# Strassen's seven products in the feed-forward part of the last two token blocks of a decoder layer

## The chip, the core and the metric

The kernel runs on one core of a Trainium2 chip. Its time is device microseconds of one execution. TensorE (PE) multiplies, VectorE (DVE), ScalarE (ACT) and GpSimd (POOL) work element by element, and every transfer is issued by SyncE (SP), one instruction after the other. Each engine takes its instructions in the order in which the program has them.

## What is computed

One decoder layer on 2048 tokens of width 1024, in float32:

```python
h = rms_norm(x, pre_mix_norm)
q, k, v_a, u, v_s = split(h @ w_in)                  # 512 columns each
attn = dilated_mixture_attention(rotary(q), rotary(k), v_a)
sgu = spatial_gating(u, v_s, ...)
y = concatenate([rms_norm(attn), rms_norm(sgu)]) @ w_out
x = x + rms_norm(y, post_mix_norm)
h = rms_norm(x, pre_ffn_norm)
f = (silu(h @ w_gate) * (h @ w_up)) @ w_down         # 1024 -> 2816 -> 1024
x = x + rms_norm(f, post_ffn_norm)
```

## The kernel before

Tokens are worked on in four blocks of 512 (m = 0 to 3). Every matrix product is made three times over in a reduced float format, `F32R`: an operand is split into a high part (a copy that rounds, on ACT) and a low part (what is left, a subtraction on DVE), and high by high, high by low and low by high are added up in PSUM. So each step of 128 in the contraction costs three matmuls of 128x512 where one would do otherwise. `wtile` (L143) loads 256 KB of a weight and splits it: `w_raw` has 3 buffers, `w_hi` and `w_lo` have 4 (`W_SPL`). `group` (L180) multiplies into four PSUM banks: for each step of the contraction it loads and then multiplies for banks 0 to 3; the last `tail` steps are turned round, so that all of them are finished for bank 0, then for bank 1 and so on, and each bank is evacuated as soon as it is done.

The program has three stretches.

1. The input projections of all blocks, with the attention of blocks 0 and 1 (`heads(0)`) interleaved.
2. Output projection and feed-forward part of blocks 0 and 1, with the attention of blocks 2 and 3 (`heads(1)`) interleaved. `merge` takes steps from both generators in a fixed ratio, 318 of the one to 252 of the other. `ffn_up` (L967) writes its result to DRAM (`fD`), and `ffn_down` (L1014) reads it back and splits it (`fsplit`, L1007, two buffers) beside the weight.
3. `out_proj(2)`, `out_proj(3)`, `ffn_prep(2)`, then the feed-forward part of blocks 2 and 3 with nothing beside it but the preparation of block 3. Here the activations stay in SBUF in split form.

`out_rows` (L861) finishes a projection: each bank goes through ACT (sum of squares) and DVE (times the gain) into `y`, which has 2 buffers in all. After the second half, for each of eight tiles of 128x512 the residual `xr` is loaded, added by DVE and the row is written out. With one `xr` buffer (`XR = 1`) the next residual is asked for when the one before has been used. `out_proj(3)` uses the same `y`, `ah` and `al` buffers as `out_proj(2)`. For the last block (`late`) the residuals are loaded early and each bank's rows are finished as soon as the bank is; there `tail` is 4.

The order on each engine is made by a scheduler that follows the program and its priorities; it can move an instruction ahead of others where buffers and data allow.

Of the kernel before, what the change touches and what calls it, by code (L numbers as in the profile page):

```python
# [10 lines left out]
F32 = mybir.dt.float32  # L11
# [15 lines left out]
NFF = DFF // P  # L27
KT = DM // P
# [45 lines left out]
LATE_TAIL = 4  # L74
# [9 lines left out]
W_SPL = 4  # L84

# [8 lines left out]
class Body:  # L94
    def __init__(self, tc, ctx, t):
# [3 lines left out]
        self.psd = ctx.enter_context(tc.tile_pool(name="psd", bufs=4, space=PSUM))  # L99
        self.psq = ctx.enter_context(tc.tile_pool(name="psq", bufs=2, space=PSUM))  # L100
        self.psv = ctx.enter_context(tc.tile_pool(name="psv", bufs=2, space=PSUM))
        self.wp = ctx.enter_context(tc.tile_pool(name="wp", bufs=1))
        self.tiny = ctx.enter_context(tc.tile_pool(name="tiny", bufs=1))
# [10 lines left out]
        self.fD = [d.tile([NFF, P, TB], F32, name=f"fD{m}") for m in range(NM)]  # L114
# [14 lines left out]
    def rstd(self, ss, n, inv_n, eps, name, parts=P):  # L129
        v = self.nc.vector  # L130
        a = self.tiny.tile([parts, n], F32, name=name + "_a", tag="rs_a", bufs=2, padded_shape=[P, 32])
        y = self.tiny.tile([parts, n], F32, name=name + "_y", tag="rs_y", bufs=6, padded_shape=[P, 32])
# [10 lines left out]
    def wtile(self, src, perm=False, shape=None, save=None, pool=None, bufs=None):  # L143
# [3 lines left out]
        raw = self.wp.tile([P, 512], F32, name="w_raw", tag="w_raw", bufs=W_RAW)  # L147
# [17 lines left out]
    def wcached(self, src, saved, perm):  # L165

        raw = self.wp.tile([P, 512], F32, name="w_raw", tag="w_raw", bufs=W_RAW)
# [56 lines left out]
    def consts(self, pool):  # L224
        self.cst = self.const.tile([P, C_TRIL], F32, name="cst")
        self.cs0 = pool.tile([P, C_W - C_TRIL], F32, name="cs0")
        self.dma(self.cs0, self.t["consts"][:, C_TRIL:C_W])
# [139 lines left out]
    def ip_keep(self, m):  # L367

        for k in range(KT):
            for i in range(2):  # L370
                self.dma(self.hD[k, i], self.h[m][i][k])
                yield
        self.dma(self.cst, self.t["consts"][:, 0:C_TRIL])
# [166 lines left out]
    def attn_pools(self, pool):  # L540
        self.ap = pool

# [314 lines left out]
    def ff_pools(self, pool, fpool):  # L857
        self.fp = pool
        self.fpool = fpool

    def out_rows(self, m, n_k, load, ops, res, gain, dst, keep, late=False):  # L861

        nc, v, pool = self.nc, self.nc.vector, self.fp
        y = [pool.tile([P, 4, 512], F32, name="y", tag="y", bufs=2) for _ in range(2)]
# [9 lines left out]
        todo = [(n, j) for j in range(4) for n in range(2)] if late else [(n, j) for n in range(2) for j in range(4)]  # L874

        def fetch(i):
            if i < 8:
                n, j = todo[i]
                tag, bufs = ("ah", KT) if late else ("xr", XR)
                xs[i] = pool.tile([P, 512], F32, name="xr", tag=tag, bufs=bufs)  # L880
                self.dma(xs[i], res[j * P:(j + 1) * P, 512 * n:512 * n + 512])

        def row(i, r):
# [6 lines left out]
            if not late:  # L890
                fetch(i + XR)

        if late:
            for i in range(8):
                fetch(i)
        for n in range(2):
            def evac(b, ps, n=n):
                nc.scalar.activation(self.junk, ps, AF.Square, accum_out=ss[:, n, b:b + 1])
                v.tensor_tensor(y[n][:, b, :], ps, grow[n], ALU.mult)  # L899
                if late and n == 1:  # L900
                    v.tensor_tensor(ss[:, 0, b:b + 1], ss[:, 0, b:b + 1], ss[:, 1, b:b + 1], ALU.add)
                    r = self.rstd(ss[:, 0, b:b + 1], 1, 1.0 / DM, RMS_EPS, "po")
                    row(2 * b, r)
                    row(2 * b + 1, r)

            yield from self.group(n_k, lambda k, n=n: load(k, n), ops, evac, tail=LATE_TAIL if late and n == 1 else 2)
        if not late:
            for i in range(XR):
                fetch(i)
            v.tensor_tensor(ss[:, 0, :], ss[:, 0, :], ss[:, 1, :], ALU.add)  # L910
            r = self.rstd(ss[:, 0, :], 4, 1.0 / DM, RMS_EPS, "po")
            for i, (n, j) in enumerate(todo):
                row(i, r[:, j:j + 1])
        if keep:
            v.tensor_tensor(sk[:, 0, :], sk[:, 0, :], sk[:, 1, :], ALU.add)
            r1 = self.rstd(sk[:, 0, :], 4, 1.0 / DM, RMS_EPS, "pk")
            self.r1[m] = self.tiny.tile([P, 4], F32, name="r1", tag="r1", bufs=NM)
            v.tensor_copy(self.r1[m], r1)
        yield

    def ffn_mid(self, m, nxt):

        if nxt is None:
            yield from self.ffn_down(m)
        else:
# [240 lines left out]
```

## Time and profile before

| | |
|---|---|
| median of 3 runs | 2553.68 us (2550.77 to 2557.73) |
| profiled execution | 2557.3 us, span 2555.5 us |
| PE busy | 2384.9 us (93% of the span), 10817 matmuls |
| DVE busy | 1551.2 us (61%) |
| ACT busy | 1156.2 us (45%) |
| POOL busy | 52.2 us (2%) |
| DMA | 439.36 MB, mean 172 GB/s |
| mean granted clock of PE | 0.964 |

The span runs from the first to the last instruction of the profiled execution. The granted clock is the share of TensorE's 2.4 GHz that the throttle let through; 0.5 of it is the lower of its two levels, 1.2 GHz. Matmuls overlap, so the length of one in a row (0.39 us) is more than the distance from one start to the next.

### The profile page before, as it was taken

What the parts mean: (1) busy time and instruction counts of PE and PEld (TensorE: products, weight loads), DVE (VectorE), ACT (ScalarE), POOL (GpSimd) and SP (SyncE); (2) the same over time, 40 slices, a digit from 0 to 9 for tenths busy, and PEclk for the clock granted to TensorE, in tenths of its full rate; (3) what the DMA queues carried; (4) which work ended last, traced back from release to release, by engine and by line L of the source; (5) the groups of instructions that cost most, each with busy time, mean ns of one, the idle gap of its engine ahead of it and who ended that gap; (6) DMA issues with size and microseconds to landing.
All of it is one profiled execution on the core that took longest, in us unless ns stands there. A gap on an engine that the chain in (4) does not pass through costs nothing.

```text
span 2555.5 us, 32840 instructions
## 1 busy us (share of the span) xinstructions
PE 2384.9 (93%) x10817; PEld 1940.0 (76%) x10817; DVE 1551.2 (61%) x3249; ACT 1156.2 (45%) x2095; POOL 52.2 (2%) x174
## 2 busy tenths in 40 slices
PE   7998869889897999999999999986999999999998
PEld 6776758767675788887788888775788888888886
DVE  5427788885786995768888575664533323533323
ACT  6425755664544653445545354443533323333321
POOL 0000000000000000000000000000000000000000
PEclk9998979889998999999999999998999999999999
DMA  7877757777866654566665445665633323533432
GB/s 243 294 218 240 224 166 225 250 219 240 259 187 182 211 159 139 142 193 184 190 202 146 125 136 178 192 218 174 185 96 95 95 92 114 157 94 95 126 101 91
DMA packets 336251, 439.36 MB, mean 172 GB/s; under 512 B 29488, under 2 KB 187728, under 8 KB 335568
## 3 DMA queue, kind: packets, MB, share of 16 engines
q1 hardware_dynamic: 336080, 437.27, 55.9%
q8 instruction: 85, 1.39, 0.2%
q14 instruction: 86, 0.70, 0.1%
HBM read 359.35 MB, written 77.80 MB: 171 GB/s over the span
## 4 chain that ended last, share of the span: by engine, by line
PE 74%; DVE 9%; DMA 9%; ACT 4%; SPq 2%; issue 2%; DVEq 0%; ACTq 0%; POOL 0%
PE d L188 67%; SPq L127 2%; DMA xr<-in_x 2%; PE qk L704 2%; PE qk L705 1%; PE pv L787 1%; PE pv L785 1%; DMA w_raw<-in_w_in 1%; DVE w_lo L160 1%; DVE y L886 1%; DVE io L427 1%; DMA xs<-in_x 1%; DMA xr<-x 1%; PE qk L313 1%; DMA w_raw<-in_w_out 0%
## 5 line engine op out<-in xcount | busy, mean ns | idle before, releaser
L160 DVE TENSOR_TENSOR w_lo<-w_raw,w_hi 128x512 fp32r<-128x512 f32 x632 | 434.1, 688 | 579.9 <-ACT w_hi L159 577.7
L159 ACT CAST w_hi<-w_raw 128x512 fp32r<-128x512 f32 x632 | 390.5, 619 | 711.0 <-PE d L188 615.0
L188 PE MATMUL d<-ah,w_hi 128*128 128x512 f32 x1408 | 556.5, 396 | 2.1 <-ACT ah L315 2.1
L188 PE MATMUL d<-ah,w_lo 128*128 128x512 f32 x1408 | 556.8, 395 | 0.0
L188 PE MATMUL d<-al,w_hi 128*128 128x512 f32 x1408 | 556.6, 395 | 0.0
L188 PEld LDWEIGHTS d<-ah,w_hi 128*128 128x128 f32 x1408 | 264.2, 188 | 62.1 <-ACT ah L315 2.6
L188 PEld LDWEIGHTS d<-ah,w_lo 128*128 128x128 f32 x1408 | 264.3, 188 | 61.6
L188 PEld LDWEIGHTS d<-al,w_hi 128*128 128x128 f32 x1408 | 264.4, 188 | 60.7
L188 PE MATMUL d<-w_hi,fh 128*128 128x512 f32 x704 | 279.4, 397 | 1.8 <-ACT fh L1011 1.8
L188 PE MATMUL d<-w_hi,fl 128*128 128x512 f32 x704 | 275.7, 395 | 3.8 <-DVE fl L1012 3.8
L188 PE MATMUL d<-w_lo,fh 128*128 128x512 f32 x704 | 278.6, 396 | 0.0
L188 PE MATMUL d<-w_hi,hh 128*128 128x512 f32 x384 | 155.5, 411 | 7.2 <-DVE io L427 5.0
L188 PEld LDWEIGHTS d<-w_hi,fl 128*128 128x128 f32 x704 | 132.1, 189 | 35.0 <-DVE fl L1012 6.8
L188 PEld LDWEIGHTS d<-w_hi,fh 128*128 128x128 f32 x704 | 133.4, 189 | 31.6 <-ACT fh L1011 3.5
L188 PE MATMUL d<-w_lo,hh 128*128 128x512 f32 x384 | 156.2, 407 | 0.0
L188 PEld LDWEIGHTS d<-w_lo,fh 128*128 128x128 f32 x704 | 133.4, 190 | 28.2
L188 PE MATMUL d<-w_hi,hl 128*128 128x512 f32 x384 | 154.3, 404 | 0.0
L188 PE MATMUL d<-w_hi,ah 128*128 128x512 f32 x256 | 105.7, 414 | 35.9 <-DVE y L899 35.9
L810 DVE TENSOR_TENSOR pl<-S,ph 128x512 fp32r<-128x512 f32 (+1 forms) x160 | 99.2, 624 | 45.3 <-ACT ph L809 26.5
L785 PE MATMUL pv<-ph,v 128*128 128x256 f32 (+1 forms) x344 | 95.4, 293 | 30.5 <-ACT ph L809 22.7
L808 ACT ACTIVATE S<-S 128x512 f32<-128x512 f32 (+1 forms) x160 | 89.5, 579 | 50.6 <-DVE S L800 43.4
L188 PE MATMUL d<-hh,w_hi 128*128 128x512 f32 x256 | 103.0, 407 | 9.6 <-DVE io L427 7.8
(206 smaller groups left out, 3623.4 us busy)
## 6 DMA issues: line engine op xcount, KB each, us to landing
w_raw<-in_w_gate SPq DMA_DIRECT2D x176, 256.0 KB
w_raw<-in_w_up SPq DMA_DIRECT2D x176, 256.0 KB
w_raw<-in_w_down SPq DMA_DIRECT2D x176, 256.0 KB
w_raw<-in_w_in SPq DMA_DIRECT2D x136, 256.0 KB
w_lo<-wc SPq DMA_DIRECT2D x96, 256.0 KB
araw<-fD SPq DMA_DIRECT2D x88, 256.0 KB
w_raw<-in_w_out SPq DMA_DIRECT2D x64, 256.0 KB
ks<-kT SPq DMA_DIRECT2D x96, 128.0 KB
```

The source lines that it names most:

```text
L127: self.nc.sync.dma_start(out, in_)
L159: nc.scalar.copy(hv, rv)
L160: nc.vector.tensor_tensor(lv, rv, hv.bitcast(F32), ALU.subtract)
L188: nc.tensor.matmul(banks[b], lhsT, rhs, start=(k == 0 and j == 0), stop=(k == nk - 1 and j == len(ops) - 1))
L313: nc.tensor.transpose(ps[:, j * P:(j + 1) * P], xs[n][:, j, c:c + P], self.ident)
L427: v.tensor_tensor(olv, src, ohv.bitcast(F32), ALU.subtract)
L704: nc.tensor.matmul(o, u[0], qh, start=True, stop=False)
L705: nc.tensor.matmul(o, u[0], ql_, start=False, stop=True)
L785: nc.tensor.matmul(ov, vv, sl(ph), start=(cnt == first[b]), stop=False, skip_group_check=True)
L787: nc.tensor.matmul(ov, vv, sl(pl), start=False, stop=(cnt == last[b]), skip_group_check=True)
L808: nc.scalar.activation(s[:, :w], s[:, :w], AF.Exp, scale=0.125)
L810: v.tensor_tensor(pl[:, o:o + w], s[:, :w], ph[:, o:o + w].bitcast(F32), ALU.subtract)
```

## The change

Blocks 2 and 3 are taken together as two columns of a 2x2 block matrix, and each large product of their feed-forward part is made of seven products of quarter matrices, in Winograd's form of Strassen's scheme, where the plain scheme has eight. The sums that this needs are made on POOL and DVE.

- `out_proj(2)` and `out_proj(3)` run ahead of the down projection of block 1. Block 3's projection has its own `ah`, `al` and `y` in a new pool `ob`, and both read their residuals through eight buffers.
- The down projection of block 1 (`d1`) is no longer interleaved with attention. Beside it, from its tenth step on, `st_prep` makes the seven right operands (`th`, `tl`, in split form, all kept in SBUF). After 20 of its steps the first gate weights are loaded (`st_first`).
- `merge` for `heads(1)` now has 269 steps against 252.
- `st_up` and `st_down` take the place of `ffn_up` and `ffn_down` of blocks 2 and 3. `st_up` also makes the sums of `w_down` and writes them (`tS`), and writes the seven left operands for the down projection (`fS`). `st_down` loads both operands of a step and splits both.
- The tail of the last product is 2 steps where the last group had 4. The PSUM pools are closed after block 1's down projection and one of six banks (`psf`) is opened.

The core of the diff (new functions shortened):

```diff
-        ffx = ExitStack()
+        ffx, fax = ExitStack(), ExitStack()
-        b.ff_pools(ff, None)
-        merge(chain(b.out_proj(0), b.out_proj(1), b.ffn_prep(0), b.ffn_up(0), b.ffn_mid(0, 1), b.ffn_up(1),
-                    b.ffn_mid(1, None)), 294 + 24, heads(1), (8 * 29 + 1) * R2)
+        b.ff_pools(ff, fa, ff, (ff, "xr", 1))
+        merge(chain(b.out_proj(0), b.out_proj(1), b.ffn_prep(0), b.ffn_up(0),
+                    _merge(b.ffn_down(0), 49, b.ffn_prep(1), 12), b.ffn_up(1)), 269, heads(1), (8 * 29 + 1) * R2)
         atx.close()
-        drain(b.out_proj(2), b.out_proj(3), b.ffn_prep(2))
-        b.ff_pools(ff, ff2)
-        drain(b.ffn_up(2), b.ffn_mid(2, 3), b.ffn_up(3), b.ffn_mid(3, None))
+        with tc.tile_pool(name="ob", bufs=1, side="right") as ob:
+            b.ff_pools(ff, fa, ff, (ob, "xr", 8))
+            drain(b.out_proj(2))
+            b.ff_pools(ff, ob, ob, (ob, "xr", 8))
+            drain(b.out_proj(3))
...
+            d1 = b.ffn_down(1)
+            drain(islice(d1, ST_AT))
+            sp = b.st_prep(pp)
+            merge(d1, 49 - ST_AT, chain(islice(sp, 20), call(b.st_first), sp), 29)
...
+                drain(b.st_up(up, us))
...
+            drain(b.st_down(dn))
+    def gain_b(self, i, ps, slot, b=None):
...
+            if i == 1:
+                nc.scalar.copy(A, ps)
+            elif i == 2:
+                v.tensor_tensor(E, ps, A, ALU.add)
+            elif i == 5:
+                nc.scalar.copy(B, ps)
+            elif i in (6, 4):
+                v.tensor_tensor(A, ps, A, ALU.add)
+            elif i == 3:
+                v.tensor_tensor(D, ps, A, ALU.add)
+                q.tensor_tensor(D, D, B, ALU.add)
+            else:
+                v.tensor_tensor(A, ps, A, ALU.add)
+                q.tensor_tensor(B, B, A, ALU.add)
+    def st_up(self, pool, spool):
...
+        for g in range(NG):
+            for n in range(2):
...
+                    q.tensor_tensor(s1, a21, a22, ALU.add)
+                    q.tensor_tensor(s2, s1, a11, ALU.subtract)
+                    q.tensor_tensor(s4, a12, s2, ALU.subtract)
+                    q.tensor_tensor(s3, a11, a21, ALU.subtract)
...
+                for i in PROD:
+                    hi, lo = self.split(left[i])
...
+                    for k in range(4):
+                        for n, (a, b) in enumerate(((hi, h), (hi, l), (lo, h))):
+                            nc.tensor.matmul(ps, a[:, c], b, start=(k == 0 and n == 0), stop=(k == 3 and n == 2))
+                    self.gain_b(i, ps, lambda n: slots[n])
...
+                    v.tensor_tensor(b11, b12, b11, ALU.subtract)
+                    v.tensor_tensor(b12, b22, b12, ALU.subtract)
+                    v.tensor_tensor(b22, b22, b11, ALU.subtract)
+                    v.tensor_tensor(b21, b21, b22, ALU.subtract)
...
+            for gt, up in zip(*both):
+                nc.scalar.activation(gt, gt, AF.Silu)
+                v.tensor_tensor(up, gt, up, ALU.mult)
...
+            q.tensor_tensor(s1, a21, a22, ALU.add)
+            q.tensor_tensor(s2, s1, a11, ALU.subtract)
+            q.tensor_tensor(s4, a12, s2, ALU.subtract)
+            q.tensor_tensor(a21, a11, a21, ALU.subtract)
+    def st_down(self, pool):
...
+        def load(i, k):
+            r = self.rw.tile([P, 2, 512], F32, name="raw", tag="raw", bufs=F_RAW)
+            self.dma(r[:, 0], self.fS[i][k])
+            self.dma(r[:, 1], right[i](k) if i in right else self.tS[i][k])
+            return self.split(r[:, 0]) + self.split(r[:, 1])
...
+        for i in PROD:
+            banks = [self.psf.tile([P, 512], F32, name="d", tag="d", bufs=6) for _ in range(4)]
...
+            tail = [load(i, k) for k in (NG - 2, NG - 1)]
+            for b in range(4):
...
+                evac(i, b, banks[b])
```

Here `NG` is 11 (groups of 256 of the 2816 columns), `PROD` is the order (1, 2, 5, 6, 3, 7, 4), `v` is DVE and `q` is POOL. `evac` of the last product adds the bank to what lies in SBUF, takes the sum of squares, multiplies by the gain and finishes two rows.

How the instructions now stand, at three places. The first is SP's order while block 2's output projection is finished; `x_2` is the DRAM copy of the block's new residual stream, `xr` the old one, `w_raw` a weight of the next projection. Before:

```order
L127 DMA w_raw<-in_w_out 128x512
L127 DMA x_2_149<-y 128x512
L127 DMA xr<-in_x 128x512
L127 DMA xs<-x_2_149 128x512
L127 DMA w_raw<-in_w_out 128x512
```

and now:

```order
L138 DMA grow<-in_post_mix_norm 128x512
L138 DMA w_raw<-in_w_out 128x512 x2
L138 DMA raw<-in_w_gate 128x4x256
L138 DMA x_2_330<-y 128x512 x7
L138 DMA w_raw<-in_w_out 128x512
L138 DMA x_2_330<-y 128x512
```

A residual was asked for after each row that was written; now the rows are written in one run, with all residuals asked for ahead of it.

The second place is POOL in `st_up`, about one group of 256 columns (`ss` are sums of weights, `fs` the four result tiles, `fc` sums of results):

```order
L1138 TENSOR_TENSOR ss<-raw,ss 128x512
L1139 TENSOR_TENSOR ss<-raw 128x512
L1136 TENSOR_TENSOR ss<-rau 128x512
L1137 TENSOR_TENSOR ss<-ss,rau 128x512
L1058 TENSOR_TENSOR fs<-fs 128x512
L1061 TENSOR_TENSOR fs<-fs 128x512
L1138 TENSOR_TENSOR ss<-rau,ss 128x512
L1167 TENSOR_TENSOR fc<-fs 128x512
L1168 TENSOR_TENSOR fc<-fc,fs 128x512
L1170 TENSOR_TENSOR fs<-fs 128x512
L1139 TENSOR_TENSOR ss<-rau 128x512
L1169 TENSOR_TENSOR fc<-fs,fc 128x512
```

POOL had no arithmetic of this kind before; now it has sixteen additions of 128x512 in each group.

The third place is DVE in `st_up`, some three products of a group (`w_lo` is a low part, `fs<-d,fs` adds a PSUM bank to a result tile, `fs<-fs` is the gate times the up projection):

```order
L1040 TENSOR_TENSOR w_lo<-ss,w_hi 128x512
L1163 TENSOR_TENSOR fs<-fs 128x512
L1040 TENSOR_TENSOR w_lo<-rau,w_hi 128x512
L1055 TENSOR_TENSOR fs<-d,fs 128x512
L1040 TENSOR_TENSOR w_lo<-raw,w_hi 128x512
L1057 TENSOR_TENSOR fs<-d,fs 128x512
```

Splits of the next products stand between the evacuations of the ones that are being made.

## Rows read from the trace of the kernel before

**Rows 1.** The page: busy us and share of each engine; the chain by engine.

```profile
PE 2384.9 (93%) x10817; PEld 1940.0 (76%) x10817; DVE 1551.2 (61%) x3249; ACT 1156.2 (45%) x2095; POOL 52.2 (2%) x174
...
PE 74%; DVE 9%; DMA 9%; ACT 4%; SPq 2%; issue 2%; DVEq 0%; ACTq 0%; POOL 0%
```

**Rows 2.** Windows: length; PE, PEld, DVE, ACT, POOL busy (x); PEclk, DMA share, GB/s.

```profile
1276.60:1550.60 274.00, 273.28 (x1283) 224.43 (x1282) 197.29 (x414) 124.61 (x202) 5.48 (x21) 1.00 0.50 150
1550.60:1617.30 66.70, 66.43 (x309) 54.57 (x307) 38.67 (x59) 33.25 (x60) 0.79 (x4) 1.00 0.58 190
1617.30:1679.40 62.10, 61.62 (x264) 49.11 (x265) 41.60 (x75) 31.04 (x58) 0.00 (x0) 1.00 0.64 205
1679.40:1801.00 121.60, 94.25 (x393) 75.67 (x391) 63.67 (x128) 47.26 (x102) 0.00 (x0) 0.89 0.57 181
1801.00:2051.70 250.70, 249.54 (x1080) 199.61 (x1081) 100.45 (x172) 91.67 (x162) 0.00 (x0) 1.00 0.41 119
...
2423.60:2544.70 121.10, 121.10 (x530) 99.02 (x528) 39.70 (x85) 30.86 (x57) 0.00 (x0) 1.00 0.30 95
2544.70:2555.50 10.80, 0.02 (x1) 0.00 (x0) 7.14 (x29) 0.69 (x2) 0.00 (x0) 0.60 0.40 147
```

**Rows 3.** Windows of plain matmuls, PE alone: length, busy us (matmuls), PEclk, DMA share, GB/s.

```profile
1820.00:2050.00 230.00, 230.00 (x987) 1.00 0.38 111
2424.00:2544.00 120.00, 120.00 (x526) 1.00 0.30 95
1618.00:1679.00 61.00, 60.95 (x263) 1.00 0.65 207
```

**Rows 4.** Waits, 1679 to 1801 us: who for whom, total us, times, longest.

```profile
PE d L188 <- DVE y L899: 26.4, 4, 19.4
...
DVE y L886 <- DMA xr<-in_x: 17.1, 7, 3.6
```

**Rows 5.** PE's timeline after one of these waits: start, length, instruction.

```profile
1709.00 0.63 PE L188 MATMUL d<-w_lo,ah 128*128 128x512 f32 x1
1709.43 0.63 PE L188 MATMUL d<-w_hi,al 128*128 128x512 f32 x1
```

**Rows 6.** PE's timeline across the middle of block 1's down projection.

```profile
1615.11 0.28 PE L787 MATMUL pv<-pl,v 128*128 128x256 f32 x1
1615.23 0.28 PE L785 MATMUL pv<-ph,v 128*128 128x256 f32 x1
...
1616.63 0.39 PE L188 MATMUL d<-w_hi,fl 128*128 128x512 f32 x1
1617.74 0.50 PE L188 MATMUL d<-w_hi,fh 128*128 128x512 f32 x1 [0.71 <-ACT fh L1011]
```

**Rows 7.** DVE's timeline in the same place: three additions in one row.

```profile
1615.39 1.89 DVE L899 TENSOR_TENSOR y<-d,grow 128x512 f32<-128x512 f32 x3
```

**Rows 8.** POOL's timeline: a copy of 128x512 alone.

```profile
749.02 0.61 POOL L566 CAST k<-ks 128x512 fp32r<-128x512 f32 x1 [2.01 <-DMA ks<-kT]
```

**Rows 9.** POOL's and DVE's timelines where both are busy.

```profile
1171.35 3.08 POOL L566 CAST k<-ks 128x128 fp32r<-128x128 f32 x3 [44.05 <-PE qk L705]
...
1172.87 1.09 DVE L160 TENSOR_TENSOR w_lo<-w_raw,w_hi 128x512 fp32r<-128x512 f32 x1
1173.99 0.69 DVE L714 TENSOR_TENSOR S<-qk,cst 128x512 f32<-128x512 f32 x1
```

**Rows 10.** Groups of instructions, whole span: count, busy us, mean ns, idle before.

```profile
L313 PE MATMUL qk<-ident,xs 128*128 128x128 f32 x256 | 43.5, 289 | 6.6 <-ACT xs L308 2.5 <-DVE hl L316 1.9 <-DVE al L316 1.4
...
L160 DVE TENSOR_TENSOR w_lo<-w_raw,w_hi 128x512 fp32r<-128x512 f32 x632 | 434.1, 688 | 579.9 <-ACT w_hi L159 577.7 <-PE d L188 1.4
```

**Rows 11.** Windows of output projection, and of block 0's down projection; columns as rows 2.

```profile
697.00:861.60 164.60, 140.41 (x637) 113.48 (x636) 130.34 (x291) 79.97 (x157) 5.55 (x16) 0.90 0.64 188
...
1115.90:1276.60 160.70, 152.03 (x721) 124.77 (x720) 135.81 (x266) 84.39 (x152) 7.24 (x20) 0.97 0.66 199
```

**Rows 12.** DVE's timeline at the end of the program.

```profile
2550.70 1.41 DVE L886 SCALAR_TENSOR_TENSOR y<-y,po_y,xr 128x512 f32<-128x512 f32 x2
```

**Rows 13.** The page: GB/s moved in each of 40 slices of the span.

```profile
GB/s 243 294 218 240 224 166 225 250 219 240 259 187 182 211 159 139 142 193 184 190 202 146 125 136 178 192 218 174 185 96 95 95 92 114 157 94 95 126 101 91
```

More of the change, by code (lines that the diff above doesn't have):

```diff
@@ L84 @@
 W_SPL = 4
+ST_AT = 10
+F_RAW = 4
+F_SUM = 6
+F_OUT = 10
+F_CMB = 4
 C_S4A = 0
@@ L854, in attn_norm, with ff_pools, out_rows @@
         yield
[L857 to L861, printed above, removed]
+    def ff_pools(self, pool, apool, ypool, xr):
+        self.fp, self.fa, self.yp, self.xr = pool, apool, ypool, xr
+    def out_rows(self, m, n_k, load, ops, res, gain, dst, keep):
         nc, v, pool = self.nc, self.nc.vector, self.fp
-        y = [pool.tile([P, 4, 512], F32, name="y", tag="y", bufs=2) for _ in range(2)]
+        y = [self.yp.tile([P, 4, 512], F32, name="y", tag="y", bufs=2) for _ in range(2)]
         ss = self.tiny.tile([P, 2, 4], F32, name="ssy", tag="ssy", bufs=3)
@@ L873, in out_rows @@
         xs = {}
-        todo = [(n, j) for j in range(4) for n in range(2)] if late else [(n, j) for n in range(2) for j in range(4)]
+        todo = [(n, j) for n in range(2) for j in range(4)]
+        ahead = self.xr[2]
         def fetch(i):
@@ L889, in row @@
                 nc.scalar.activation(self.junk, yj, AF.Square, accum_out=sk[:, n, j:j + 1])
[L890 to L895, printed above, removed]
+            fetch(i + ahead)
         for n in range(2):
@@ L899, in evac @@
                 v.tensor_tensor(y[n][:, b, :], ps, grow[n], ALU.mult)
[L900 to L913, printed above, removed]
+            yield from self.group(n_k, lambda k, n=n: load(k, n), ops, evac)
+        for i in range(ahead):
+            fetch(i)
+        v.tensor_tensor(ss[:, 0, :], ss[:, 0, :], ss[:, 1, :], ALU.add)
+        r = self.rstd(ss[:, 0, :], 4, 1.0 / DM, RMS_EPS, "po")
+        for i, (n, j) in enumerate(todo):
+            row(i, r[:, j:j + 1])
         if keep:
@@ L999, in evac @@
                     ff = 2 * g + b % 2
-                    if self.fpool is not None:
-                        self.fsplit(ff, s, self.fpool, NFF)
-                    else:
-                        self.dma(self.fD[m][ff], s)
+                    self.dma(self.fD[m][ff], s)
             yield from self.group(KT // 2, load, feat, evac, tail=1)
@@ L1031, in ffn_down, with split @@
         rows = slice(m * TB, (m + 1) * TB)
-        yield from self.out_rows(m, NFF, load_d, ops, self.x1[m], "post_ffn_norm", t["out"][0, rows], False,
-                                 m == NM - 1)
+        yield from self.out_rows(m, NFF, load_d, ops, self.x1[m], "post_ffn_norm", t["out"][0, rows], False)
+    def split(self, src):
+        nc = self.nc
+        hi = self.wp.tile([P, 512], F32R, name="w_hi", tag="w_hi", bufs=W_SPL)
+        lo = self.wp.tile([P, 512], F32R, name="w_lo", tag="w_lo", bufs=W_SPL)
+        hv, lv = hi, lo
+        if len(src.shape) == 3:
+            hv, lv = (t.rearrange("p (a b) -> p a b", a=src.shape[1]) for t in (hi, lo))
+        with self.tc.high_priority(HP_W):
+            nc.scalar.copy(hv, src)
+            nc.vector.tensor_tensor(lv, src, hv.bitcast(F32), ALU.subtract)
+        return hi, lo
@@ new lines, in gain_b @@
+    def gain_b(self, i, ps, slot, b=None):
+        nc, v, q = self.nc, self.nc.vector, self.nc.gpsimd
+        A, B, D, E = (slot(n) for n in range(4))
+        with self.tc.high_priority(HP_E):
+            if i == 1:
[9 more added lines that the diff above has]
+                q.tensor_tensor(D, D, B, ALU.add)
+            else:
+                v.tensor_tensor(A, ps, A, ALU.add)
+                q.tensor_tensor(B, B, A, ALU.add)
@@ new lines, in st_raw, with st_first @@
+    def st_raw(self, g, n, pool):
+        w = self.t[("w_gate", "w_up")[n]][0].rearrange("(k p) c -> p k c", p=P)
+        r = []
+        for j in range(2):
+            r.append((pool.tile([P, 1024], F32, name="raw", tag="raw", bufs=F_RAW) if n == 0 else
+                      pool.tile([P, 1024], F32, name="rau", tag="rau", bufs=2)).rearrange("p (k c) -> p k c", k=4))
+            self.dma(r[j], w[:, 4 * j:4 * j + 4, 256 * g:256 * g + 256])
+        return r
+    def st_first(self):
+        self.raw0 = self.st_raw(0, 0, self.rw)
```

192 lines of the change are left out of this document (161 added, 31 removed).

## The prediction

> **What bounds the kernel now.** The page first: PE is busy for 93% of the span and the chain that ended last is PE for 74% [rows 1]. That is an average over stretches with different limits, so the windows come next [rows 2]. From 1801.0 us to 2544.7 us, the feed-forward part of blocks 2 and 3, PE is busy all the time at full granted clock, while DVE works 100 us of 250 in the first stretch: there only fewer matmuls, or cheaper ones, can save time. What a matmul costs is read where nothing else runs [rows 3]: 230.0/987 = 0.233 us in the up projection, 120.0/526 = 0.228 us in block 3's down projection, and 61.0/263 = 0.232 us in block 1's, where both operands of a step are loaded and split as it goes. None of the three needs more than the clock gives; where two operands are split at 205 GB/s, the pace holds as well.
>
> The stretch from 1679.4 us to 1801.0 us is different: PE busy 94.25 of 121.6 us, clock 0.89 [rows 2]. The waits name the place [rows 4]: PE waits 26.4 us in four waits for `y`, the evacuation of a bank, since the two `y` buffers are held until the rows of the projection before are out, and these wait for residuals that come one by one (17.1 us). After such a wait the starts are 0.43 us apart [rows 5], as at the lower clock, until the clock comes back.
>
> **The change part by part.** The sum is made against the span of 2555.5 us. The profiled execution took 2557.3 us, 3.6 us more than the median of the three runs; the difference is carried to the median.
>
> *Matmuls.* The scheme makes seven products of eight. The up projections had 2 x 1056 matmuls and have 1848; the down projections had 2 x 528 and have 924. Up: 1848 x 0.233 = 430.6 us. Down: both operands are now split as in block 1, so 924 x 0.232 = 214.4 us. To this come two losses.
>
> Between two products of the down projection the split buffers are all held by the turned-round tail. In block 1's down projection the same buffers meet the same tail, and there the next start comes 1.11 us after the last instead of 0.23 [rows 6]. Six such borders at 0.88 us are 5.3 us.
>
> At the start of `st_up` the result tiles lie where `y` of block 1 lay, which is free only when its last rows are out. The last bank's way out took 10.8 us at the end of the program [rows 2]; six PSUM banks hold six products of 12 x 0.233 = 2.8 us, 16.8 us. So the banks mostly cover it; between nothing and 10.8 us I take 5, since ACT and DVE take splits in the same queue as the evacuations.
>
> Together 655.3 us where 743.7 us were (2544.7 - 1801.0): **-88.4 us**.
>
> *The cover in `st_up`.* A group has 2 x 7 x 12 = 168 matmuls, 39.1 us. DVE has 14 splits, 10 evacuations, 4 sums of `w_down` and 4 products with the gate: 32 operations. Three in a row take 1.89 us [rows 7], so 0.63 us each and 20.2 us in all. POOL has 16 additions. Before, POOL adds nothing; its nearest row is a copy of 128x512, 0.61 us alone [rows 8], with one operand where an addition has two. I take twice that, 1.2 us, 19.2 us in all. Either engine alone is hidden.
>
> But they get in each other's way. Three copies that take 0.61 us at the most alone needed 3.08 us together while DVE worked, and the subtraction of two SBUF operands beside them took 1.09 us, where the addition of a mask to a PSUM bank right after took its 0.69 us although POOL was still at it [rows 9]. Of the 32 DVE operations 22 read two SBUF operands: 22 x 0.63 + 19.2 = 33.1 us if these never overlap with POOL, still under 39.1 us; if no DVE operation at all overlapped it would be 39.4 us, 0.3 us too much in each of 11 groups. I cost it at nothing; the splits run up to four products ahead (`w_hi` has four buffers).
>
> The Trainium skill says the same more strictly (SBUF — State Buffer, "Who interferes with whom"): the second DVE port is GpSimd's, the lock is exclusive and held for a whole instruction, and a DVE instruction with two SBUF inputs contends with a GpSimd instruction that reads SBUF. The stretched subtraction agrees with it. By this rule the 22 and the 16 never overlap, which is the 33.1 us above and leaves the sum as it is; what it adds is that the loser waits for a whole instruction, so that the price of an addition under load, which no row has, decides.
>
> *Output projections of blocks 2 and 3.* Own `y`, `ah` and `al` and eight residual buffers take away what PE waited for [rows 4]. 384 matmuls x 0.233 = 89.5 us, and 1 us for their beginning, in place of 121.6 us: **-31.1 us**. If the waits stay, nothing of it.
>
> *Block 1's down projection.* It moves behind them, alone on PE but for `st_prep`. It took 128.8 us with the rest of the attention beside it [rows 2]. Now: 528 x 0.232 = 122.5 us, the border in its middle 0.9 us, and 64 transposes at 43.5/256 = 0.17 us [rows 10], 10.9 us, together 134.3 us: **+5.5 us**. DVE has 41.6 of 62.1 us there now, 67%; 16 products and 28 splits at 0.63 us add 28 us, some 82% in all. That is what the first down projection has (84.5% [rows 11]), so up to 10 us may be lost; I take none. The transposes were done before too, in the stretches that are gone.
>
> *The attention of blocks 2 and 3* loses cover. 45 of its matmuls stood beside block 1's down projection (309 - 264 [rows 2]); at 0.12 us each [rows 6] that is 5.4 us of PE time that moves ahead. More: in PE's order as built, the first 480 matmuls of output projection and feed-forward work have 180 attention matmuls between them where there were 134; later the counts are alike, until the attention ends three groups before `ffn_up(1)` does. What one attention matmul brings to DVE follows from `ffn_up(1)`: 197.3 us of DVE less 11 groups of 10 operations at 0.688 us [rows 10], over 1283 - 1056 = 227 matmuls [rows 2], 0.54 us. So 46 more bring 25 us of DVE work into a stretch where DVE is busy 130.3 of 164.6 us [rows 11] and PE already loses a few per cent. If the idle fifth takes it, the cost is the 5.4 us of PE time; if DVE stays at its share, 25/0.79 = 31 us. Between these I take 18 us, and 3 us for the other denser places: **+21 us** (5 to 40).
>
> *The end.* After the last matmul 10.8 us were left, most of it DVE, whose last rows end 3.4 us before the span does [rows 12]. With a tail of two steps the banks come 6 x 0.23 = 1.4 us apart and not 2.8, so DVE begins three times 1.4 us later against PE's end, and each of four banks needs one more addition: 4.2 + 2.5 = **+6.7 us**.
>
> *Transfers.* `st_down` loads 512 KB for each 2.8 us, 188 GB/s, under the 205 GB/s of block 1's [rows 2]. While product 7 is made the rows of block 2 come to it, 8 x 512 KB: 10 MB in 30.8 us. The fastest slice of the page moved 294 GB/s [rows 13], by which this would take 34 us. Up to 3 us, costed at nothing.
>
> Sum: -88.4 - 31.1 + 5.5 + 21 + 6.7 = -86.3 us. Span 2469.2 us, and from the median 2553.7 - 86.3 = **2467 us**.
>
> **The rivals.**
>
> *The waits only move.* PE still waits in the output projections, since the gain row `grow` has one buffer and the rows of one block still come late, and the attention costs its upper bound: 26 + 19 us more, **2512 us**. For it: these two stretches lose most time now, and denser attention work in front of the same DVE speaks for new waits. Against it: eight residuals are asked for well ahead. That the new buffers don't do what they are said to is part of this case.
>
> *POOL and DVE fill the group in part.* At 1.45 us an addition and no overlap, 23.2 + 20.2 = 43.4 us for a group instead of 39.1: 11 x 4.3 = 47 us more, **2514 us**. For it: the sum has no room above 1.2 us if nothing overlaps.
>
> *They bound it outright: slower than before.* Each addition waits for DVE as the copies did: 3.08/3 = 1.03 us for one operand [rows 9], 2.05 for two. 16 x 2.05 + 20.2 = 53.0 us for a group, 13.9 us over PE's time, 153 us in eleven groups: **2620 us**. It decides against the change from 7.8 us a group on, that is (39.1 + 7.8 - 20.2)/16 = 1.67 us an addition. Against it: DVE's evacuations read PSUM and leave POOL alone, and DVE waits for PE part of the time.
>
> *Nothing of the losses comes.* Attention at its lower bound, no late start, no longer end, borders covered: 16 + 5 + 7 + 5 = 33 us less, **2434 us**.
>
> **How the numbers follow.** Forecast 0.60, the waits move 0.15, POOL in part 0.10, no losses 0.09, POOL outright 0.06. All but the last are faster by more than 0.3% (7.7 us), which is about what a measurement of this kernel can tell from no change; 0.03 of them I set aside for two of the middle cases coming together, 2560 us, about no change. So faster 0.91, same 0.03, slower 0.06. The range reaches from the forecast with small losses to the two middle cases with the bounds of the output projection: 2437 to 2528 us.
>
> **What would show it.** Right: 396 matmuls fewer, a pace of 0.233 us in `st_up`, PE's waits for `y` gone between the output projections, borders of about 1.1 us in `st_down`, additions on POOL of 1.2 us or less. Wrong: a group of `st_up` of clearly more than 39 us with PE waiting for `w_lo` or `w_hi`; DVE above 90% with PE idle in the first feed-forward stretch; granted clock under 1 anywhere after 1600 us.

## The result and the profile after

The changed kernel takes 2528.37 us (median of 4 runs, 2527.41 to 2529.09) where the kernel before took 2555.70 us in the runs beside it. The ratio is 0.9896, 95% interval 0.9868 to 0.9924: 1.0% faster, where 3.4% was forecast. The time lies 61 us above the forecast and just outside its range (2437 to 2528 us). The profiled execution has a span of 2526.3 us, against 2469.2 us in the sum.

The first lines of the page of the changed kernel, which answer to [rows 1]:

```profile
span 2526.3 us, 32789 instructions
...
PE 2300.0 (91%) x10421; PEld 1870.8 (74%) x10421; DVE 1774.3 (70%) x3437; ACT 1170.3 (46%) x2141; POOL 369.3 (15%) x386
```

396 matmuls have gone, as forecast, and yet PE's share fell: there are new waits. The windows by stretch (columns as in [rows 2]) say where. They run from the first matmul of a stretch to the first of the next: output projections of blocks 0 and 1 to block 1's up projection; output projections of blocks 2 and 3; block 1's down projection with `st_prep`; `st_up` in two pieces; `st_down`; the end.

```profile
690.50:1553.50 863.00, 815.80 (x3873) 673.23 (x3873) 665.95 (x1406) 416.27 (x718) 23.37 (x83) 0.97 0.56 169
1553.50:1653.20 99.70, 92.53 (x385) 73.57 (x386) 56.14 (x106) 44.10 (x94) 0.00 (x0) 0.97 0.77 223
1653.20:1802.30 149.10, 134.33 (x593) 108.07 (x591) 108.05 (x174) 75.56 (x148) 23.46 (x16) 0.97 0.60 187
1802.30:2038.40 236.10, 206.10 (x840) 162.74 (x841) 168.03 (x204) 62.98 (x111) 122.16 (x81) 0.94 0.57 195
2038.40:2269.20 230.80, 230.80 (x1010) 189.46 (x1009) 152.99 (x170) 76.55 (x133) 136.97 (x91) 1.00 0.30 98
2269.20:2508.80 239.60, 224.73 (x925) 176.72 (x923) 136.81 (x197) 99.83 (x188) 35.50 (x25) 0.96 0.58 189
2508.80:2526.30 17.50, 0.17 (x1) 0.00 (x0) 12.21 (x63) 1.37 (x4) 0.00 (x0) 0.62 0.50 180
```

| stretch | forecast, us | measured, us | miss |
|---|---|---|---|
| before the output projections | 697.0 | 690.5 | -6.5 |
| to the end of `ffn_up(1)`, 853.6 + 21 | 874.6 | 863.0 | -11.6 |
| output projections 2 and 3 | 90.5 | 99.7 | +9.2 |
| block 1's down projection, `st_prep` | 134.3 | 149.1 | +14.8 |
| `st_up`, 430.6 + 5 | 435.6 | 466.9 | +31.3 |
| `st_down`, 214.4 + 5.3 | 219.7 | 239.6 | +19.9 |
| the end | 17.5 | 17.5 | 0 |

The misses add up to the 57 us between the two spans. The first row says nothing of the change: in the twelve profiles of the changed kernel and its variants, which all have that part alike, it took 686.0 to 697.5 us. In `st_up` the miss lies in the first five groups: the second half of it, six groups, has PE busy in every microsecond, 230.8 us at full clock, though POOL is busy for 137 us of it.

Two places of the trace show what PE waited for. At the start of `st_up` it stood twice (start, length, instruction, idle time before it and what ended it). The first wait ends where `st_up` is counted from, so its 4.05 us lie in the row of block 1's down projection:

```profile
1802.32 0.50 PE L1149 MATMUL d<-th,w_hi 128*128 128x512 f32 x1 [4.05 <-DVE y L907]
...
1820.11 0.80 PE L1149 MATMUL d<-th,w_hi 128*128 128x512 f32 x1 [10.42 <-ACT w_hi L1039]
```

Between the two lie 24 matmuls, two products. They run partly 0.43 us apart, as at the lower clock. The waits of the other engines there name block 1's outgoing rows:

```profile
POOL ss L1136 <- DMA out<-y: 17.8, 1, 17.8
ACT fs L1049 <- DMA out<-y: 16.5, 1, 16.5
...
DVE y L898 <- DMA xr<-x: 4.7, 4, 1.6
```

After that, from 1825 to 2038 us, PE waits 14 times for a low part (`w_lo`), while DVE waits for the weights of the sums of `w_down`, and POOL for the up projection's weights:

```profile
POOL ss L1136 <- DMA rau<-in_w_up: 31.5, 4, 10.9
...
DVE wd L1155 <- DMA wd<-in_w_down: 24.3, 9, 5.3
PE d L1149 <- DVE w_lo L1040: 19.5, 14, 2.6
DVE fs L1163 <- POOL fs L1058: 18.1, 4, 5.7
```

All 44 sums of `w_down` were made in this piece, those of eleven groups in the time of five: their one buffer is free as soon as its sums are written out, so the next load and the next sums start at once, whether PE has come that far or not.

### The profile page after: what moved, and what is told of

It reads as the page before. It is cut to its first block, busy times and chain, and to the rows that moved or that the text cites. A ratio compares the mean times of both kernels' runs of the same rounds, so it can differ in the third digit from the quotient of the medians.

```text
span 2526.3 us, 32789 instructions
## 1 busy us (share of the span) xinstructions
PE 2300.0 (91%) x10421; PEld 1870.8 (74%) x10421; DVE 1774.3 (70%) x3437; ACT 1170.3 (46%) x2141; POOL 369.3 (15%) x386
## 5 line engine op out<-in xcount | busy, mean ns | idle before, releaser
L171 DVE TENSOR_TENSOR w_lo<-w_raw,w_hi 128x512 fp32r<-128x512 f32 x368 | 255.9, 698 | 190.0 <-ACT w_hi L170 178.9
L170 ACT CAST w_hi<-w_raw 128x512 fp32r<-128x512 f32 x368 | 227.1, 618 | 316.7 <-PE d L199 245.8
L199 PE MATMUL d<-al,w_hi 128*128 128x512 f32 x704 | 276.6, 393 | 0.0
L199 PE MATMUL d<-ah,w_lo 128*128 128x512 f32 x704 | 276.2, 392 | 0.0
L199 PE MATMUL d<-ah,w_hi 128*128 128x512 f32 x704 | 276.0, 393 | 0.0
L1149 PE MATMUL d<-th,w_lo 128*128 128x512 f32 x616 | 245.5, 399 | 19.6 <-DVE w_lo L1040 19.5
L1149 PE MATMUL d<-th,w_hi 128*128 128x512 f32 x616 | 245.3, 398 | 14.5 <-ACT w_hi L1039 10.4
L1149 PE MATMUL d<-tl,w_hi 128*128 128x512 f32 x616 | 245.9, 399 | 0.0
L1040 DVE TENSOR_TENSOR w_lo<-raw,w_hi 128x512 fp32r<-128x512 f32 x187 | 149.1, 831 | 93.2 <-ACT w_hi L1039 92.3
L199 PE MATMUL d<-w_lo,fh 128*128 128x512 f32 x352 | 140.1, 398 | 0.0
```

Source lines behind the costliest of these rows:

```text
L170: nc.scalar.copy(hv, rv)
L171: nc.vector.tensor_tensor(lv, rv, hv.bitcast(F32), ALU.subtract)
L199: nc.tensor.matmul(banks[b], lhsT, rhs, start=(k == 0 and j == 0), stop=(k == nk - 1 and j == len(ops) - 1))
L1040: nc.vector.tensor_tensor(lv, src, hv.bitcast(F32), ALU.subtract)
L1149: nc.tensor.matmul(ps, a[:, c], b, start=(k == 0 and n == 0), stop=(k == 3 and n == 2))
```

## The experiments

A comparison between kernels rests on the ratio to the kernel before (the changed kernel: 0.9896) and on the length of one stretch in the profile. Only the intervals of experiments 1, 2 and 8 and of the second kernel of 6 lie clear of that of the changed kernel, 0.9868 to 0.9924; for the others the stretch decides, and it is read from one profile each. Where an experiment leaves a stretch as it is, the profiles have 99.7 to 102.1 us for the two projections, 148.1 to 149.4 for block 1's down projection, 466.5 to 469.8 for `st_up` and 235.7 to 239.6 for `st_down`. Theories: **A**, sums of `w_down` that run ahead block the orders of DVE, SP and POOL; **B**, POOL and DVE lock each other out of SBUF; **C**, DVE is full or transfers late; **D**, SP stands at residual loads; **E**, the start of `st_up` waits for block 1's rows; **F**, a write in pieces of 4 bytes holds up all transfers.

### 1. The sums of w_down held to their group

```diff
                 v.tensor_tensor(up, gt, up, ALU.mult)
+            pc = self.tiny.tile([P, 1], F32, name="pc", tag="pc", bufs=1)
+            v.tensor_tensor(pc, wr[:, 1, 1023:1024], both[1][3][:, 0:1], ALU.add)
```

> Same work; one tiny DVE addition per group (about 0.1 us each, 1 us in all) holds the one `wd` buffer until the group's last product with the gate, so the four sums of w_down can no longer run a group ahead. Theory A (the sums and their loads run ahead and block DVE's, SP's and POOL's orders while the first five groups are made): `st_up` falls from 466.8 us to about 440 us, what is left of the loss is the start; DVE's 24.3 us of waits for `wd` go; the whole about 2500 us. Theory B (POOL and DVE lock each other out of SBUF, so every group with its full share of DVE work loses): the sums now fall into the groups that lost nothing, these lose 1 to 4 us each, `st_up` stays within 5 us of 466.8 and the whole at 2525 to 2532 us.

2507.75 us, ratio 0.9815 (0.9786 to 0.9844). `st_up` took 447.9 us in place of 466.9. After its start it runs at PE's pace (the whole of it, then without its start; columns as above):

```profile
1803.10:2251.00 447.90, 436.75 (x1848) 349.10 (x1849) 355.78 (x383) 140.47 (x244) 272.45 (x172) 0.98 0.45 154
1860.00:2251.00 391.00, 390.34 (x1671) 312.79 (x1670) 314.69 (x327) 126.39 (x220) 245.51 (x155) 1.00 0.44 148
```

390.34 of 391 us, with the same sums and POOL busy for 246 us. Theory A holds: a group with its full share of work takes 39.2 us (39.1 forecast). The lock of theory B is there, but costs nothing here. From 1860 us on the splits of sums take 1.12 us on average, where a split alone takes 0.69 [rows 10], and PE hardly waits for a low part:

```profile
L1040 DVE TENSOR_TENSOR w_lo<-ss,w_hi 128x512 fp32r<-128x512 f32 x79 | 88.0, 1116 | 21.6 <-ACT w_hi L1039 21.1
...
PE d L1149 <- DVE w_lo L1040: 0.7, 2, 0.3
```

### 2. The sums left out

```diff
-                    v.tensor_tensor(b11, b12, b11, ALU.subtract)
-                    v.tensor_tensor(b12, b22, b12, ALU.subtract)
-                    v.tensor_tensor(b22, b22, b11, ALU.subtract)
-                    v.tensor_tensor(b21, b21, b22, ALU.subtract)
```

> The four sums of w_down are left out in every group (its quarters are loaded and written to `tS` as they are, so four of the right operands of the down projection are not the scheme's): DVE has 44 operations less, SP still issues all loads and writes of `wd` and they still run ahead. If the loss in the first groups of `st_up` is DVE's (44 x 0.69 = 30 us of work and 24.3 us of waits for `wd` in its order): `st_up` falls from 466.8 us to about 445 us, as with the held sums. If it is SP's (the load of `rau` stands behind `tS` and `wd` in its order, and POOL's sums and all behind them wait for it): `st_up` stays at 460 to 470 us, with POOL still waiting over 20 us for `rau`.

2509.92 us, ratio 0.9835 (0.9815 to 0.9854); `st_up` 450.2 us. POOL waited longer for `rau` than before:

```profile
POOL ss L1136 <- DMA rau<-in_w_up: 66.5, 6, 19.0
...
PEld d L1149 <- DVE w_lo L1040: 10.9, 5, 4.4
```

So the loads and writes that run ahead in SP's order, which this kernel keeps, are not what cost most. 16.7 of the 19.0 us went with the sums on DVE, their waits for `wd` included. How much of it was the order alone and how much the operations that the lock stretches is not separated. POOL's wait for `rau`, though among the longest in the list, costs PE only the few gaps that are left.

### 3. Block 1's rows and the start of `st_up`

First, all eight residuals are asked for before the first row, four of them in one load into `qd`, a buffer that `st_prep` has just left:

```diff
+                if self.xq is not None and n == 0:
+                    if j == 0:
+                        xq = self.xq.tile([P, 4, TB], F32, name="qd", tag="qd", bufs=1)
+                        self.dma(xq, res.rearrange("(j p) c -> p j c", p=P)[:, :, 0:512])
...
```

> Block 1's rows: four of the eight residuals are loaded at once into the buffer that `st_prep` has just left, the other four as before, so all eight are asked for before the first row and no load stands between the rows. Theory E (the tiles of `st_up` wait for block 1's last rows, which come one residual after the other): the two gaps of 4.4 and 10.8 us at the start of `st_up` shrink to 3 to 6 us in all, `st_up` falls from 466.8 us to about 457 us, the whole to about 2518 us. Rival (the first sums on POOL and the loads behind them come late anyway): the gaps stay at about 15 us in all, `st_up` within 3 us of 466.8, the whole 2525 to 2531 us.

2522.38 us, ratio 0.9864 (0.9836 to 0.9891), `st_up` 463.0 us. PE's two waits became 4.0 and 6.1 us, 10.1 in all where 14.5 were (the expectations count them at the weight load, 4.4 and 10.8 us): the residuals were 4.4 us of it, nearly a third. The interval overlaps that of the changed kernel; the stretch shows the change, the whole hardly.

Then, on top of it, `y` was moved:

```diff
+        yb = yfx.enter_context(tc.tile_pool(name="yb", bufs=1, side="left"))
-        b.ff_pools(ff, None, ff, (ff, "tmp", 4))
+        b.ff_pools(ff, None, yb, (ff, "tmp", 4))
```

> Block 1's rows as in the kernel that loads all eight residuals at once; besides, `y` gets a pool of its own above the other buffers of that stretch, so that the first result tiles `fs` of `st_up` no longer lie over it. Theory E (product 1's way out waits for `out<-y`, and ACT's splits wait behind it): the gap of 6.5 us that was left at the start goes to 1 to 2 us, `st_up` falls from 463.0 us to about 458 us, the whole to about 2517 us. Rival (POOL's first sums `ss` wait for the same rows and are what PE needs): the gap stays at 5 us or more, `st_up` within 2 us of 463.0, the whole about 2522 us.

2524.83 us, ratio 0.9872 (0.9831 to 0.9914), waits of 4.0 and 6.0 us, `st_up` 462.4 us: nothing gained. The waits still name the same rows (`ACT fs <- DMA out<-y`, 12.1 us), so the place of `y` within the memory was not enough. The next kernel, on top of both, has pools of its own for what must start early, and loads `wd` behind `rau`:

```diff
-            with tc.tile_pool(name="us", bufs=1, side="right") as us:
-                drain(b.st_up(up, us))
+            with tc.tile_pool(name="us", bufs=1, side="right") as us:
+                with tc.tile_pool(name="up2", bufs=1, side="left") as up2:
+                    with tc.tile_pool(name="us2", bufs=1, side="right") as us2:
+                        drain(b.st_up(up, us, up2, us2))
```

> As the kernel with `y` above the other buffers, and the tiles of `st_up` stand in four pools in place of two, so that the pools of the first result tiles `fs` and of the first sums `ss` no longer lie over a pool that block 1's outgoing rows hold (the `wd`, `rau` and `fc` tiles do). Theory E (what PE waits for at the start is the way out of block 1's rows; moving `y` alone did not help because the first tile of a pool waits for all that lay in the closed pools under it): the gap of 6.4 us goes to under 2 us, `st_up` falls from 462.4 us to 456 to 459 us, the whole to about 2518 us. Rival (ACT and DVE finish block 1's evacuation and rows first, in their own order): the gap stays within 1.5 us of 6.4, the whole about 2523 us.

2519.90 us, ratio 0.9850 (0.9821 to 0.9879), `st_up` 460.8 us. The wait for `out<-y` is gone from the list; in its place stand these:

```profile
POOL ss L1145 <- DVE y L907: 12.4, 1, 12.4
...
ACT fs L1059 <- issue: 6.7, 1, 6.7
```

PE's waits are 4.0, 5.0 and 1.6 us, 10.6 in all, no better. By its numbers the rival came about, and DVE does go through evacuations, factor and eight rows first. But the trace also shows what POOL's first sum waits for, the last row that takes its residual from `qd`:

```profile
1810.72 2.07 DVE L907 SCALAR_TENSOR_TENSOR y<-y,po_y,qd 128x512 f32<-128x512 f32 x3
...
1813.01 1.26 POOL L1145 TENSOR_TENSOR ss<-raw 128x512 f32<-128x512 f32 x1 [12.39 <-DVE y L907]
```

`qd` belongs to the pool `pp`, which is closed just before the pool of `ss` is opened on the same side. So part of the wait is likely one that the first of these edits made itself; no run has the residuals elsewhere. E is right about what is waited for, block 1's rows, and 4.4 us of the 14.5 were removed.

### 4. POOL's work in `st_prep` and in `st_down` on DVE

```diff
-            q.tensor_tensor(b11, b12, b11, ALU.subtract)
+            v.tensor_tensor(b11, b12, b11, ALU.subtract)
...
```

> In `st_prep` the 16 subtractions of `qd` go from POOL to DVE (16 x 0.69 = 11 us more DVE work in a stretch where DVE is some 80% busy); POOL has nothing left there. Theory B (the lock with POOL stretches the splits, and `fl` waits behind them): block 1's down projection falls from 149.2 us to 139 to 142 us, the gaps of 1.6 to 3.1 us go, the whole about 2520 us. Theory C (DVE is simply full there, or the transfers are late): the stretch stays at 148 to 155 us, the whole 2527 to 2534 us.

2516.80 us, ratio 0.9852 (0.9819 to 0.9885); block 1's down projection took 139.4 us in place of 149.1, as theory B has it, although DVE now does more. PE's waits for `fl` fell from 9.3 us to 2.9. (Some 2 us of the gain went on: PE's second wait at the start of `st_up` grew from 10.4 to 12.7 us.) The groups of DVE's instructions (count, busy us, mean ns) there, in the changed kernel:

```profile
L1007 DVE TENSOR_TENSOR fl<-araw,fh 128x512 fp32r<-128x512 f32 x42 | 32.0, 764 | 28.3 <-ACT fh L1006 26.3 <-PE qk L1102 1.0 <-PE d L199 0.9
...
L1087 DVE TENSOR_TENSOR tl<-qd,th 128x512 fp32r<-128x512 f32 x27 | 22.6, 867 | 4.1 <-ACT th L1086 4.1
```

and with POOL idle:

```profile
L1007 DVE TENSOR_TENSOR fl<-araw,fh 128x512 fp32r<-128x512 f32 x42 | 28.8, 689 | 19.7 <-ACT fh L1006 16.7 <-PE qk L1102 2.9
...
L1087 DVE TENSOR_TENSOR tl<-qd,th 128x512 fp32r<-128x512 f32 x26 | 17.4, 686 | 3.9 <-ACT th L1086 3.9
```

The same for `st_down`:

```diff
-            (v if i == 4 else q).tensor_tensor(c, c, grow[:, n, :], ALU.mult)
+            v.tensor_tensor(c, c, grow[:, n, :], ALU.mult)
...
```

> In `st_down` the eight additions and twelve products with the gain that POOL makes go to DVE (20 x 0.69 = 14 us more for DVE in 240 us); POOL has nothing left there. Theory B (the lock with POOL stretches the four splits at a border): the two borders of 2.4 us fall to about 0.7 us and the gaps of 2.1 to 2.8 us go; `st_down` falls from 239.8 us to about 231 us, the whole to about 2519 us. Theory C (the refill of four split buffers or the transfers are late, whoever adds): borders and gaps stay, `st_down` within 3 us of 239.8 or longer by part of the 14 us.

2518.33 us, ratio 0.9851 (0.9810 to 0.9891); `st_down` took 229.7 us in place of 239.6, so 6 to 10 us less by the spread given above. At the border into product 7, the changed kernel's DVE (first line) and POOL (the others), and then DVE of the experiment at the same border:

```profile
2433.36 6.76 DVE L1040 TENSOR_TENSOR w_lo<-raw,w_hi 128x512 fp32r<-128x512 f32 x4 [0.78 <-ACT w_hi L1039]
...
2434.47 1.73 POOL L1213 TENSOR_TENSOR sl<-sl,gr 128x512 f32<-128x512 f32 x1
2436.17 1.72 POOL L1058 TENSOR_TENSOR sl<-sl 128x512 f32<-128x512 f32 x1
```

```profile
2428.22 2.50 DVE L1040 TENSOR_TENSOR w_lo<-raw,w_hi 128x512 fp32r<-128x512 f32 x4
2430.63 1.90 DVE L1213 TENSOR_TENSOR sl<-sl,gr 128x512 f32<-128x512 f32 x3
```

Four splits in 6.76 us beside POOL, in 2.50 us without. The other borders agree: in the changed kernel PE waits 0.3 to 0.4 us at the three that have POOL at rest, and 2.7, 3.2 and 3.7 us at the three where POOL works; with that work on DVE these three have 1.0, 2.0 and 2.9 us. B holds at these two places, where the splits lie on PE's path.

### 5. The residuals of block 3 in their own buffers

```diff
-            b.ff_pools(ff, ob, ob, (ob, "xr", 8))
+            b.ff_pools(ff, ob, ob, (ob, "xr3", 8))
```

> Block 3's output projection reads its residuals into eight buffers of its own. Theory D (SP stood 10 us at residual loads whose buffers block 2's rows still held, and the weights behind them came late): the gap of 5.76 us in block 3's projection goes, both projections take about 95 us in place of 100.8, the whole about 2522 us. Rival (ACT and DVE prepare block 3's left operand ahead of block 2's evacuations, and that makes the gaps): both projections stay within 2 us of 100.8, the whole 2526 to 2531 us.

2530.64 us, ratio 0.9895 (0.9874 to 0.9916); both projections 105.7 us, worse than 99.7. D falls: no residual load stood in SP's order there, and PE's longest wait was 7.9 us. The transfers of this run from 1615 to 1640 us, in 40 slices (busy tenths; GB/s), show something else:

```profile
DMA  9968996842200004242234223876999998999999
GB/s 380 400 207 344 331 187 229 315 167 8 24 24 0 0 0 54 50 36 30 35 38 31 29 34 50 129 205 219 291 360 345 246 167 218 347 385 375 338 372 393
```

From 1621 us on, right after SP issued `rR<-pk_y` at 1620.2, little moves for 10 us. The changed kernel has the same twice, after each of its two writes of this kind (512 pieces of 4 bytes, 2 KB in all); after the first of them transfers come back for about one microsecond before the long slump. From 1612 to 1632 us and from 1674 to 1694 us:

```profile
GB/s 397 385 283 315 393 307 229 229 299 205 131 7 30 123 332 270 78 20 12 41 16 16 20 12 12 12 4 53 25 53 143 209 188 193 229 168 201 291 213 225
```

```profile
GB/s 251 195 229 320 290 304 301 279 185 141 270 135 8 0 20 61 66 33 45 37 33 45 12 53 147 123 115 152 287 254 315 311 397 397 402 406 209 172 66 299
```

### 6. The factors written in rows of 128 bytes

```diff
-                self.dma(self.rR[m].rearrange("(j p) -> p j", p=P), r1)
+                v.tensor_copy(w[:, 0:4], r1)
+                v.transpose(u, w)
+                for q in range(4):
+                    self.dma(self.rR[m].rearrange("(j b c) -> b j c", b=4, c=32)[q], u[32 * q:32 * q + 4])
```

> The factors `r1` of blocks 2 and 3 are turned in SBUF (one DVE transpose) and written to `rR` as 16 rows of 128 bytes, where the changed kernel writes 512 pieces of 4 bytes. Theory F (after such a write all transfers stand still for some 7 us, as the trace shows twice: 12 to 48 KB per us where 300 to 400 moved before): the two slumps go, both projections take about 94 us in place of 99.7, block 1's down projection 3 to 7 us less than 149.2, the whole about 2517 us. Rival (the slump comes from SP, which stands at residual loads, or from the reads of what was just written): slumps and stretches stay within 2 us, the whole 2526 to 2531 us.

2515.39 us, ratio 0.9842 (0.9811 to 0.9873). The projections took 93.0 us, block 1's down projection 144.3 us: F holds. From 1612 to 1632 us:

```profile
GB/s 377 369 270 303 377 221 217 180 348 377 299 95 1 2 0 164 287 270 340 176 225 283 279 365 406 410 401 402 352 229 164 201 246 254 315 377 336 389 365 365
```

The slump of six to seven microseconds has become one of about two. With this, and block 3's own residual buffers as well:

> The 128-byte rows for `rR` together with the eight own residual buffers of block 3's projection. Alone the first took the two projections from 99.7 to 92.9 us, the second to 105.6 us. If the own buffers lost because the load of the weights then ran into the slump at another place, without the slump both projections take 91 to 94 us. If they lose by themselves (the residuals come early and push weights back), 97 us or more.

2513.73 us, ratio 0.9846 (0.9826 to 0.9865), projections 94.6 us. The own buffers lost only together with the slump, and are worth nothing without it.

### 7. One part of the change alone, in the kernel before

```diff
+        with tc.tile_pool(name="ob", bufs=1, side="right") as ob:
+            b.ob = ob
+            drain(b.out_proj(2), b.out_proj(3))
+            b.ob = None
...
```

> The kernel before with one part of the change alone: block 3's output projection gets its own `ah`, `al` and `y`, both projections eight residual buffers; the rest, with the factors kept in SBUF, is as before. By the forecast's term the stretch of 121.6 us becomes 90.5 us and the whole some 2524 us. By theory F the same, since there is no 4-byte write here. If the own buffers are worth only what the changed kernel shows (121.6 to about 100 us), the whole is about 2534 us.

2541.63 us, ratio 0.9935 (0.9911 to 0.9959). The two projections took 104.0 us in place of the 121.6 us of [rows 2]. Of the four waits in [rows 4] one long one is left, and the residuals that come one by one:

```profile
PE d L188 <- DVE y L903: 13.1, 2, 12.4
...
DVE y L890 <- DMA xr<-x: 7.1, 3, 3.9
```

These are block 1's rows, which hold the `y` that block 2 shares with it. In the changed kernel block 1's down projection comes later, and its rows hold up `st_up` instead. By the names of the waits, this one was moved.

### 8. The repairs together

The edits of 1, 3 (all three), 4 (both) and 6.

> All repairs together: the sums of w_down held to their group, POOL's subtractions of `st_prep` and its additions and products of `st_down` on DVE, the rows of 128 bytes for `rR`, and the start as in the kernel with four pools. If the losses add up: 2528.4 less 21 (pace), 10 (`st_down`), 10 (`st_prep`), 11 (`rR`) and 6 to 12 (start) gives 2464 to 2470 us, beside the 2467 us once forecast. If they cover one another (DVE full where it now does POOL's work, the start late for another reason): 2480 to 2495 us.

2480.66 us, ratio 0.9707 (0.9682 to 0.9732), 48 us less than the changed kernel and the fastest of all. Output projections, block 1's down projection, `st_up` and `st_down`:

```profile
1553.90:1645.80 91.90, 89.86 (x384) 71.86 (x385) 56.39 (x108) 44.10 (x94) 0.00 (x0) 1.00 0.74 242
1645.80:1780.20 134.40, 129.84 (x594) 106.17 (x592) 105.58 (x190) 75.26 (x148) 0.00 (x0) 0.99 0.66 208
1780.20:2228.40 448.20, 437.44 (x1849) 349.17 (x1850) 354.11 (x385) 140.33 (x244) 271.97 (x172) 0.98 0.45 153
2228.40:2458.60 230.20, 218.73 (x925) 173.41 (x923) 134.91 (x217) 99.89 (x188) 6.36 (x5) 0.99 0.62 197
```

The whole came out between the two expectations, 2464 to 2470 and 2480 to 2495 us, at the edge of the second. By stretches the repairs add up, 7.8 + 14.7 + 9.4 us and 18.7 in `st_up`, but for the start: PE's waits there are 2.1, 6.8 and 2.8 us, and `st_up` is as long as with the held sums alone.

## Why the prediction was wrong

Two of the prediction's own signs of being wrong came: groups of clearly more than 39 us with PE waiting for `w_lo`, in the first half of `st_up`, and a granted clock of 0.94 to 0.97 after 1600 us.

*Matmuls* held: 10421 of them, and 39.2 us for a group at full clock.

*The cover in `st_up`* was the step that failed most. "I cost it at nothing" compared sums of work per group, and these were right: POOL's additions take 1.26 to 1.29 us alone where 1.2 was estimated, and held to their group, all the work is covered (experiment 1). What was not looked at is when the work comes. Nothing ties the sums of `w_down` to their group but one buffer; those of eleven groups were made while PE made five, and stood in front of what PE needed. That is some 19 of the 31 us.

*The late start* ("between nothing and 10.8 us I take 5") was mis-sized: 15 us. By experiment 1 the first 177 matmuls of `st_up` took 447.9 - 391.0 = 56.9 us where 0.233 us each make 41.2; 10.5 us of the difference is PE's wait, and the rest are matmuls further apart, at a mean granted clock of 0.85. Less the 5 us taken, this and the 19 us make up 30 of the 31.3. "Six PSUM banks hold six products" is true, but the third product needs a sum that POOL makes, and POOL waited as well; PE stopped after two products. 4.4 us of the wait were the residuals; the rest was not brought down by any run here.

*Borders of the down projection* (5.3 us) and *block 1's down projection* ("up to 10 us more may be lost; I take none") left out that the lock with POOL, which [rows 9] showed, matters most in the short stretches where a split is on PE's path. It cost 9.7 us in block 1's down projection and 6 to 10 in `st_down` (experiment 4). The prediction weighed it only for `st_up`, where it costs nothing. The Trainium skill (SBUF — State Buffer, "Who interferes with whom") has the lock exclusive and held for whole instructions. The traces agree with it roughly: 6.76 us for four splits beside about four POOL operations, where strictly one after the other these would need 2.50 + 4 x 1.27 = 7.6 us.

*Output projections* (-31.1 us) came to -21.9 us. The waits for `y` between the projections did go; what came was the write in pieces of 4 bytes, 6.7 us here and 4.8 us in the next stretch. The prediction listed *Transfers* by bytes and costed 2 KB at nothing.

*The attention*, +21 us within 5 to 40, measured +9.4, and 4 to 10 over the twelve profiles. *The end*, +6.7 us, was exact in its number, in part by luck: the last rows waited 1.14 and 1.01 us for residuals, which the term does not have. The rival that the waits only move named 2512 us; its mechanism was there for one wait, at another place. The other two on POOL did not come about: under load an addition takes 1.58 us on average (experiment 1, 245.51/155), more than the 1.45 of the milder one and more than the 1.2 that the prediction named as its sign of being right, yet PE is busy all through the groups.

Open: what would clear the remaining 10 us at the start of `st_up`, and 10 us in `st_down` beyond its term after the repair, with waits of up to 2.6 us at the borders and beside the rows. Shorter rows of block 1, finished bank by bank, were not tried.

## What to carry to other kernels

Work beside a bottleneck that fits by its sum must also come at its time: tie what can be made early (a single buffer that frees itself is no tie) to the step that needs it. A second engine that helps is free where its partner has slack and dear where the partner's next result is awaited, so place it by stretch. And look at the shape of every new transfer, however few its bytes.

## What was not expected of the hardware

A write of 512 pieces of 4 bytes to DRAM, 2 KB, was followed by six to ten microseconds in which the transfers behind it moved less than 80 GB/s, mostly 10 to 50, in place of 200 to 400, three times in the two traces shown, while the DMA engines counted as busy for a part of it; the same 2 KB in 16 pieces of 128 bytes cost about two. And DVE did its own and POOL's work sooner than its own alone beside POOL: `st_down` took 229.7 us with 20 operations more on DVE, 235.7 to 239.6 us with them on POOL.
